# A decoder layer in fp32: two groups of attention steps placed later in a written schedule

## The chip, the cores and the metric

The kernel runs on one core of one Trainium2 chip. The metric is the device time of one execution in microseconds (us): the median of several runs. The core has five engines that run beside each other and wait for one another by semaphores: TensorE (PE, with its weight loads as PEld), VectorE (DVE), ScalarE (ACT), GpSimd (POOL) and SyncE (SP), which here issues nearly all of the transfers.

## The reference

One layer of a decoder on 512 tokens of width 2048, all in fp32:

```
h    = rms_norm(x, norm1_g)
proj = h @ w_in                     # split into aq ak av | bu bg | cq ck cv
out_a = dilated_mixture(rms(aq), rms(ak), av)       # 8 heads x 64, three (window, dilation) patterns
out_b = conformer_conv(bu, bg, ...)                 # GLU, causal conv of 31, layer norm, silu
out_c = band_attention(rms(cq), rms(ck), cv, 127, sinks)   # 16 query heads, 2 kv heads, x 64
x = x + concat(out_a, out_b, out_c) @ w_out
h2 = rms_norm(x, norm2_g)
x = x + (silu(h2 @ w_gate) * (h2 @ w_up)) @ w_down
```

Both attentions are softmax(q k) v with a mask. The C heads see a window of 128 tokens and have a sink in the denominator. The A heads see all 512 tokens through one mask whose entries count how many of the three patterns hold a pair.

## The kernel before

Every fp32 product is made of three products of split operands: high times high, high times low, low times high. A weight comes in by DMA, ACT rounds it to its high part (wh, line 289), and DVE subtracts to get its low part (wl, line 263).

The work goes in stages: the input projection (30 column tiles, named in the list PROJ), the output projection (16 tiles in two halves of the rows, ROWS), and the feed-forward part, which takes most of the time. The attention and the convolution are not stages of their own. They are strewn over the input projection and the first half of the output projection, so that PE has the projection's matmuls to do while the other engines work on the heads.

What is strewn where is written out by hand with a counter of ticks. The class Ticks keeps a list of functions due at each tick. project() calls ticks.tick() after every two steps of the contraction, that is after every six matmuls, so a column tile has eight ticks; a tile of the first half of the output projection has four. Each tick issues what is due at it, in the order in which it was entered, into the queues of the engines. Every engine then works through its own queue in that order. A step that is due a tick later thus stands behind some six more matmuls in PE's queue, and behind what the other engines were given in that tick.

The function attention(kind, box, mix, mi, heads) enters the steps of two heads for each query tile. Its distances in ticks come from the two tuples C_TICKS and A_TICKS, unpacked in one line:

```python
ready, every, step, s1, sx, s2, fl, ev, we = C_TICKS if kind == "c" else A_TICKS
if mi in ROWS[-2:]:
    fl, we = fl + 2, we + 3
at_v = (len(us) - 1) * step + s1 + sx + s2 + fl + len(TBANKS[kind]) - 1 + ev + EV + we
t0 = max(ticks.now + ready, head_at[0], box["q at"] - s1, box["k at"], box["v at"] - at_v)
ticks.after(tu + s2 + fl, packed_flip)        # C
ticks.after(tu + s2 + fl + t, flip, t)        # A, t = 0, 1, 2
ticks.after(t0 + at_v, weigh)
```

A head starts at t0, and the next one `every` ticks later: six for C, eight for A. The steps of a head are:

- scores (lines 814 and 815): q times k, on PE, in two (C) or three (A) PSUM banks, `step` ticks apart
- pack or top (820 to 829, 880 to 883): masks and maxima, on DVE; then exps (835, 889) on ACT and the norm (842 to 844, 896 to 900) on DVE
- flip: PE turns the normed weights, four 128x128 blocks at once for a C head (850) and 4, 4 and 2 blocks in three successive ticks for an A head (916)
- high and low: for an A head ACT casts the turned bank (922) and DVE subtracts (927); for a C head ACT and DVE do the same (856, 861), and POOL then selects the band out of both parts into four tiles ph and pl (870 and 873)
- weigh: PE multiplies with v, from ph (940) and pl (941), eight matmuls a head, into one bank
- out_high and out_rows: ACT copies one half of that bank (949) and DVE adds the other (954), one and two ticks after weigh

When both heads of a row are done, split_mix makes its high part on ACT (994) and its low part on DVE (995). The C rows are split at ticks that are set by the projection's last tiles; a row that ends after the projection is split one tick after its out_rows. For all heads but two, t0 is set by the head before or by q; for none is it set by v.

Two shared stores matter. PSUM has six banks for the scores, turns and products of all heads, and two ("tiles") for the projection's own tiles. SBUF has a pool of 73 slots of 128x512 (sp, N_SLOTS) for nearly every tile of a head. A slot is taken at the first write of a tile and given back at its last read; the next tile to be written gets the slot that came back first. If none is free, the writing engine waits for one. In the output projection the bank of a tile is freed by residual() (line 1073, xr), one tick after the tile's end.

Of the kernel before, what the change touches and what calls it, by code (L numbers as in the profile page):

```python
# [39 lines left out]
SD, KD, VD, EV = 9, 6, 12, 1  # L40


C_TICKS = (1, 6, 2, 2, 2, 3, 5, 1, 4)
A_TICKS = (0, 8, 2, 1, 3, 1, 3, 1, 5)


PROJ = ("bu0 bg0 bu1 bg1 cv ck cq0 bu2 cq3 cq1 cq5 bu3 cq2 bg2 cq7 "
# [69 lines left out]
def kernel(ctx: ExitStack, tc: tile.TileContext, xT, wi, wo, wgu, wd, cst_in, outT):  # L117
# [675 lines left out]
    def attention(kind, box, mix, mi, heads):  # L793
        ready, every, step, s1, sx, s2, fl, ev, we = C_TICKS if kind == "c" else A_TICKS

# [898 lines left out]
```

## Time and profile before

| | us |
|---|---|
| median of 3 runs | 1843.22 |
| lowest and highest run | 1843.0 and 1843.69 |
| profiled execution, its own time | 1845.39 |
| profiled execution, span from first to last instruction | 1843.6 |

| engine | busy us | share of the span |
|---|---|---|
| PE | 1835.2 | 100% |
| PEld | 1522.4 | 83% |
| DVE | 1445.8 | 78% |
| ACT | 1312.1 | 71% |
| POOL | 1026.2 | 56% |

The granted TensorE clock is 1.00. The attention lies between about 100 and 470 us of the span, the feed-forward part after 580 us.

A row of a timeline has the start and the length in us, the engine, the line, the operation, the tiles (out<-in) with their shapes, the number of instructions, and in brackets the idle time just before it with what ended it. c1o is the product with v of row c1, c1ph and c1pl its operands, a0t a turned bank of row a0, a0e its normed weights; digits of heads are left out, so both heads of a row have the same name. Matmuls overlap, so the time that one takes from the next is the distance of their starts, not the length of the row. A row of the waits has the waiting engine, tile and line, what it waited for, the sum in us, how often, and the longest.

### The profile page before, as it was taken

What the parts mean: (1) busy time and instruction counts of PE and PEld (TensorE: products, weight loads), DVE (VectorE), ACT (ScalarE), POOL (GpSimd) and SP (SyncE); (2) the same over time, 40 slices, a digit from 0 to 9 for tenths busy, and PEclk for the clock granted to TensorE, in tenths of its full rate; (3) what the DMA queues carried; (4) which work ended last, traced back from release to release, by engine and by line L of the source; (5) the groups of instructions that cost most, each with busy time, mean ns of one, the idle gap of its engine ahead of it and who ended that gap; (6) DMA issues with size and microseconds to landing.
All of it is one profiled execution on the core that took longest, in us unless ns stands there. A gap on an engine that the chain in (4) does not pass through costs nothing.

```text
span 1843.6 us, 26502 instructions
## 1 busy us (share of the span) xinstructions
PE 1835.2 (100%) x8314; PEld 1522.4 (83%) x8314; DVE 1445.8 (78%) x2063; ACT 1312.1 (71%) x1784; POOL 1026.2 (56%) x790
## 2 busy tenths in 40 slices
PE   9999999999999999999999999999999999999998
PEld 7888888888888888888888888888888888888887
DVE  6789988997689877778777787777777777777777
ACT  6345554553458788888888888888887778777775
POOL 0126644110003557886788767878676558776552
PEclk9999999999999999999999999999999999999999
DMA  7353345353343457677867778677687679877735
GB/s 276 87 150 93 87 121 153 107 161 116 124 149 103 115 151 191 188 213 182 225 187 200 201 188 226 181 209 199 182 273 258 204 225 295 257 254 260 240 119 110
DMA packets 398924, 334.61 MB, mean 181 GB/s; under 512 B 184256, under 2 KB 326720, under 8 KB 398784
## 3 DMA queue, kind: packets, MB, share of 16 engines
q1 hardware_dynamic: 398208, 332.14, 62.3%
q8 instruction: 66, 1.08, 0.3%
q10 hardware_dynamic: 576, 0.79, 0.1%
q14 instruction: 74, 0.61, 0.1%
HBM read 258.46 MB, written 65.98 MB: 176 GB/s over the span
## 4 chain that ended last, share of the span: by engine, by line
PE 95%; DVE 3%; DMA 1%; issue 0%; ACT 0%; SPq 0%; POOL 0%; DVEq 0%; POOLq 0%; ACTq 0%
PE out L1281 15%; PE out L1279 15%; PE out L1282 15%; PE out L1544 7%; PE out L1546 7%; PE out L1545 7%; PE o L322 3%; PE o L323 3%; PE o L324 3%; PE cq L322 2%; PE cq L324 2%; PE cq L323 2%; PE in L324 1%; PE in L323 1%; PE in L322 1%; PE aq L322 1%
## 5 line engine op out<-in xcount | busy, mean ns | idle before, releaser
L1279 PE MATMUL out<-wh,h 128*128 128x512 f32 x1232 | 479.2, 389 | 0.0
L1281 PE MATMUL out<-wl,h 128*128 128x512 f32 x1232 | 479.2, 389 | 0.0
L1282 PE MATMUL out<-wh,h 128*128 128x512 f32 x1232 | 479.2, 389 | 0.0
L1279 PEld LDWEIGHTS out<-wh,h 128*128 128x128 f32 x1232 | 231.2, 188 | 48.1
L1282 PEld LDWEIGHTS out<-wh,h 128*128 128x128 f32 x1232 | 231.2, 188 | 48.0
L1281 PEld LDWEIGHTS out<-wl,h 128*128 128x128 f32 x1232 | 231.2, 188 | 47.9
L1545 PE MATMUL out<-wl,a 128*128 128x512 f32 x620 | 240.4, 388 | 0.1
L1544 PE MATMUL out<-wh,a 128*128 128x512 f32 x620 | 240.4, 388 | 0.0
L1546 PE MATMUL out<-wh,a 128*128 128x512 f32 x620 | 240.3, 388 | 0.0
L289 ACT CAST wh<-w 128x1024 fp32r<-128x1024 f32 (+2 forms) x94 | 96.9, 1031 | 121.6 <-PE o L323 48.0
L1554 DVE TENSOR_TENSOR y<-y,out 128x512 f32<-128x512 f32 x192 | 128.5, 684 | 47.8 <-PE out L1546 46.1
L263 DVE TENSOR_TENSOR wl<-w,wh 128x1024 fp32r<-128x1024 f32 (+2 forms) x95 | 115.0, 1211 | 30.9 <-ACT wh L289 27.9
L1545 PEld LDWEIGHTS out<-wl,a 128*128 128x128 f32 x620 | 116.4, 188 | 24.5 <-DVE wl L285 0.5
L1546 PEld LDWEIGHTS out<-wh,a 128*128 128x128 f32 x620 | 116.4, 188 | 23.8
L1544 PEld LDWEIGHTS out<-wh,a 128*128 128x128 f32 x620 | 116.4, 188 | 23.8
L573 DVE SCALAR_TENSOR_TENSOR y<-bu,cst,y 128x511 f32<-128x511 f32 (+14 forms) x120 | 92.0, 767 | 1.3
L322 PE MATMUL o<-mh_c,wh 128*128 128x512 f32 x128 | 51.1, 399 | 0.2 <-DVE xr L1073 0.2
L322 PE MATMUL cq<-hh,wh 128*128 128x512 f32 x128 | 50.3, 393 | 0.0
L324 PE MATMUL o<-mh_c,wl 128*128 128x512 f32 x128 | 50.0, 391 | 0.0
L323 PE MATMUL o<-ml_c,wh 128*128 128x512 f32 x128 | 50.0, 390 | 0.0
L323 PE MATMUL cq<-hl,wh 128*128 128x512 f32 x128 | 49.9, 390 | 0.0
L324 PE MATMUL cq<-hh,wl 128*128 128x512 f32 x128 | 49.9, 390 | 0.0
(2351 smaller groups left out, 4766.5 us busy)
## 6 DMA issues: line engine op xcount, KB each, us to landing
od<-a SPq DMA_DIRECT2D x154, 256.0 KB
a<-od SPq DMA_DIRECT2D x154, 256.0 KB
w<-in_wi SPq DMA_DIRECT2D x58, 512.0 KB
w<-in_wo SPq DMA_DIRECT2D x32, 512.0 KB
x<-in_xT SPq DMA_DIRECT2D x16, 256.0 KB
xr<-in_xT SPq DMA_DIRECT2D x16, 256.0 KB
x2d<-xr SPq DMA_DIRECT2D x16, 256.0 KB
z<-x2d SPq DMA_DIRECT2D x64, 64.0 KB
```

Of the source, the lines that this page charges most:

```text
L263: fn(*args)
L289: (nc.vector.tensor_copy if u == 0 else nc.scalar.copy)(hi[:, :n], t[:, :n])
L322: nc.tensor.matmul(out, wh, xh, start=start, stop=False)
L323: nc.tensor.matmul(out, wh, xl, start=False, stop=False)
L324: nc.tensor.matmul(out, wl, xh, start=False, stop=stop)
L1279: nc.tensor.matmul(b, x[:, high], wh[:, s], start=c == f == 0 and q in (7, 1, 5, 2), stop=False, skip_group_check=True)
L1281: nc.tensor.matmul(b, x[:, high], wl[:, s], start=False, stop=False, skip_group_check=True)
L1282: nc.tensor.matmul(b, x[:, low], wh[:, s], start=False, stop=c == f == 1, skip_group_check=True)
L1544: nc.tensor.matmul(b[:, lo:hi], x[:, high], wh[:, s], start=start, stop=False, skip_group_check=True)
L1545: nc.tensor.matmul(b[:, lo:hi], x[:, high], wl[:, s], start=False, stop=False, skip_group_check=True)
L1546: nc.tensor.matmul(b[:, lo:hi], x[:, low], wh[:, s], start=False, stop=last, skip_group_check=True)
L1554: getattr(eng, op)(t, t, src)
```

## The change

Two figures of the two tuples change. The last one of C_TICKS, `we`, goes from 4 to 6: the products with v of every C head, and with them out_high and out_rows, come two ticks later. (The change was described as three steps; the diff has two.) The seventh of A_TICKS, `fl`, goes from 3 to 4: the three turns of every A head come one tick later, and so does all that is counted from them: high, low, weigh, out_high, out_rows. Nothing else is touched; scores, maxima, exponentials, norms, turns of the C heads and the selects on POOL keep their ticks.

```diff
-C_TICKS = (1, 6, 2, 2, 2, 3, 5, 1, 4)
-A_TICKS = (0, 8, 2, 1, 3, 1, 3, 1, 5)
+C_TICKS = (1, 6, 2, 2, 2, 3, 5, 1, 6)
+A_TICKS = (0, 8, 2, 1, 3, 1, 4, 1, 5)
```

## The prediction

> **What bounds the kernel now.** I read the page first, for the share of the engines and for the chain, then the list of waits on TensorE, then the stages, then TensorE's timeline around each wait.
>
> ```profile
> span 1843.6 us, 26502 instructions
> PE 95%; DVE 3%; DMA 1%; issue 0%; ACT 0%; SPq 0%; POOL 0%; DVEq 0%; POOLq 0%; ACTq 0%
> ```
>
> The chain of waits lies on TensorE (PE) for 95% of the span, so only time in which PE stands still can be won, and only a new standstill of PE can cost. The whole list of what PE waited for is short:
>
> ```profile
> PE idle L348 <- DVE nhalf L352: 1.1, 1, 1.1
> PE c1o L941 <- POOL c1pl L873: 0.8, 2, 0.5
> PE sides L1509 <- DVE y L1523: 0.6, 1, 0.6
> PE in L516 <- ACT hh L402: 0.6, 1, 0.6
> PE a0t L916 <- DVE a0e L900: 0.3, 1, 0.3
> PE o L322 <- DVE xr L1073: 0.2, 1, 0.2
> PE a1t L916 <- DVE a1e L900: 0.2, 1, 0.2
> ```
>
> "idle" and "in" are the start and "sides" is the end of the kernel; no moved step is near them. The other four lie in the attention, and three of them are waits of steps that the change moves: the products with v of one C head (c1o) and the turns of two A heads (a0t, a1t). The fourth, "o", waits for a residual addition of DVE. The stage says why DVE is late there:
>
> ```profile
> 299.00:403.00 104.00, 103.39 (x508) 86.36 (x506) 96.13 (x236) 54.50 (x97) 20.76 (x32) 1.00 0.51 135
> ```
>
> The columns are length, then the busy time of PE, weight loads, DVE, ACT and POOL, the granted clock, DMA. Where the A heads begin (299 to 403 us), DVE, the fourth figure, works 96.13 of 104.00 us, so whatever DVE hands to PE there comes late.
>
> **The change part by part.** No instruction is added or removed. The words of the change say three steps for the C heads; the diff raises the last figure from 4 to 6, two ticks, and I go by the diff. For each of 16 C heads two ticks later come 8 products on PE, one copy on ACT (L949), one addition on DVE (L954). For each of 8 A heads one tick later come 10 turns on PE, three casts on ACT (L922), three subtractions on DVE (L927), then the 8 products, their copy and addition, and for a1, a2 and a3, which end late, the split of the row (L994, L995). None of these issues a DMA, so nothing is moved on SP's queue; on POOL nothing is moved either, but slots that POOL writes come free later (below). The scores, maxima, exponentials and norms keep their ticks.
>
> *The C products.* PE's timeline at both heads of c1:
>
> ```profile
> 183.55 0.28 PE L940 MATMUL c1o<-c1ph,cv 128*128 128x256 f32 x1
> 184.34 0.39 PE L941 MATMUL c1o<-c1pl,cv 128*128 128x256 f32 x1 [0.52 <-POOL c1pl L873]
> ...
> 185.77 0.45 PE L322 MATMUL cq<-hh,wh 128*128 128x512 f32 x1
> ...
> 195.41 0.28 PE L940 MATMUL c1o<-c1ph,cv 128*128 128x256 f32 x1
> ...
> 196.30 0.45 PE L322 MATMUL bg<-hh,wh 128*128 128x512 f32 x1
> ```
>
> The first head's group takes 185.77 - 183.55 = 2.22 us, the second's 196.30 - 195.41 = 0.89. The loss is 1.33 us, more than the 0.8 of the list, since that list leaves out the pipeline's refilling. The two heads lie six ticks apart: (195.41 - 183.55 - 1.33) / 6 = 1.75 us for a tick. What was late is POOL:
>
> ```profile
> 182.91 1.39 POOL L873 TENSOR_SCALAR_AFFINE_SELECT c1pl<-c1lp 128x256 fp32r<-128x256 f32 x1
> 184.25 0.82 POOL L870 TENSOR_SCALAR_AFFINE_SELECT c1pl<-c1lp 128x256 fp32r<-128x256 f32 x1
> 185.03 0.29 POOL L873 TENSOR_SCALAR_AFFINE_SELECT c1pl<-c1lp 128x128 fp32r<-128x128 f32 x1
> ```
>
> POOL's last select ends at 185.03 + 0.29 = 185.32. Two ticks later the group would start at 183.55 + 3.50 = 187.05, 1.7 us after that. So the 1.33 us go: **-1.33**. Next late would be the second head of the same pair, which already runs without a wait. The copy and the addition behind the products are needed only when the rows are split, over 20 ticks later for every C row by the code's times; that cover hides them. If it were gone, they would cost one ACT and one DVE instruction each.
>
> One of the selects took 1.39 us, its neighbour of the same size 0.82. The row that overlaps it is DVE's split of a weight, with both inputs in SBUF:
>
> ```profile
> 182.63 1.40 DVE L263 TENSOR_TENSOR wl<-w,wh 128x1024 fp32r<-128x1024 f32 x1 [0.20 <-ACT wh L289]
> ```
>
> The select ends at 184.30, 0.27 us after the split's end at 184.03. The Trainium skill, page "SBUF — State Buffer", section "Who interferes with whom", says that a VectorE instruction with two SBUF inputs keeps a GpSimd instruction that reads SBUF out altogether until it is through; these two rows agree. By that rule the selects' length depends on what DVE runs beside them and can change with any change of the alignment; what it would do here is the third rival.
>
> *The A turns.* First an undisturbed group of turns with the scores behind it, then the two late ones:
>
> ```profile
> 331.88 0.60 PE L916 MATMUL a0t<-ident,a0e 128*128 128x128 f32 x4
> 332.24 0.48 PE L814 MATMUL a0s<-ak0h,aq 128*128 128x512 f32 x1
> 332.56 0.39 PE L815 MATMUL a0s<-ak0l,aq 128*128 128x512 f32 x1
> 332.79 0.40 PE L322 MATMUL av<-hh,wh 128*128 128x512 f32 x1
> ...
> 345.23 0.49 PE L916 MATMUL a0t<-ident,a0e 128*128 128x128 f32 x3
> 346.00 0.33 PE L916 MATMUL a0t<-ident,a0e 128*128 128x128 f32 x1 [0.28 <-DVE a0e L900]
> 346.09 0.48 PE L814 MATMUL a1s<-ak1h,aq 128*128 128x512 f32 x1
> ...
> 374.21 0.49 PE L916 MATMUL a1t<-ident,a1e 128*128 128x128 f32 x3
> 374.88 0.33 PE L916 MATMUL a1t<-ident,a1e 128*128 128x128 f32 x1 [0.17 <-DVE a1e L900]
> 374.96 0.48 PE L322 MATMUL aq<-hh,wh 128*128 128x512 f32 x1
> ```
>
> Four turns take 332.24 - 331.88 = 0.36 us to the next start; at 345.23 they take 0.86 and at 374.21 0.75. The losses are 0.50 and 0.39, because PE arrives up to half a microsecond before the last norm. A tick later (1.75 us) PE arrives well over 1 us after it: **-0.89**. A cover that shrinks: the turned banks are freed by DVE's subtractions a tick later, while the scores that use the six banks next keep their ticks. No wait for a bank stands in the list now, so its cost lies between nothing and one tick (1.75); I take nothing, because the list of PE's waits has no row of that kind (for the same reason there is nothing to gain), and keep the tick for the range. Splitting a turn from the scores it shared a tick with costs little: the joint group takes 332.79 - 331.88 = 0.91. I allow 0.02 us for each of some ten new groups, from the resolution of these rows: **+0.2**.
>
> *The residual.* The bank that output tile 2 needs is freed by xr:
>
> ```profile
> 402.46 0.39 PE L815 MATMUL a2s<-ak2l,aq 128*128 128x512 f32 x1
> 403.05 0.47 PE L322 MATMUL o<-mh_c,wh 128*128 128x512 f32 x1 [0.20 <-DVE xr L1073]
> ```
>
> ```profile
> 397.90 0.69 DVE L995 TENSOR_TENSOR ml_a<-mix_a,mh_a 128x512 fp32r<-128x512 f32 x1 [0.69 <-ACT mh_a L994]
> ```
>
> The step to the next matmul is 0.59, against 332.79 - 332.56 = 0.23 undisturbed: a loss of 0.36. DVE stood 0.69 us idle ahead of ml_a, the split of row a1, which the change puts a tick later: behind the weight's split and the norm, in front of xr still. ACT's cast for it is then ready in time, DVE loses its 0.69 idle, and xr comes earlier by that. Bounds: all of the 0.36 goes, or ml_a stays late and xr comes a tick (1.75) later. I take most of it, **-0.3**, the row's 0.69 being larger than what is needed.
>
> Sum: -1.33 - 0.89 - 0.3 + 0.2 = -2.3 us. The profiled execution took 1845.39 us (span 1843.6 and 1.79 around it), so its like would take 1843.1. The median of the runs, 1843.22, is 2.17 lower; there the sum gives **1840.9 us**, 0.13% less. More than 1.33 + 0.89 + 0.36 = 2.58 us is not to be had by this change, as the list has no other wait of PE in the attention.
>
> **The rivals.**
>
> *Slots (slower).* 73 slots serve the C parts, the A exponentials and the q, k, v copies. A slot goes to the next writer in the order in which slots come free, and around the last C head and the first A head they run out:
>
> ```profile
> 328.42 0.78 ACT L889 ACTIVATE a0e<-a0s,a0d,aq0r 128x512 f32<-128x512 f32 x1 [3.90 <-PE c6o L940]
> ```
>
> ```profile
> 330.51 0.48 DVE L900 TENSOR_SCALAR a0e<-a0e,a0d 128x512 f32<-128x512 f32 x1
> ```
>
> The exponentials of A head 0 stood 3.90 us until the products of c6 freed a slot, not because they read those products. The change holds four slots and a half of v for two ticks longer just there. If the same writer gets the same slot, ACT starts 3.5 us later, DVE's norm (ending at 330.99 now) ends at 334.5, and the turns, at 331.88 + 1.75 = 333.63, wait 0.9; DVE, with no slack up to 403, carries the rest of its 3.5 us on to the later turns and to xr. PE then loses about 3.5 in that stage in place of 1.25, so the time is 1843.22 - 1.33 + 2.25 + 0.2 = 1844.3; with two writers held, 7 us instead of 3.5, 1847.8. It decides from the point where the added hold is over 2 us. Against it: counting through the code's ticks, the copy of the moved products (L949) also takes its slot two ticks later, and the freed copy of q (after L681) comes ahead of the products, so that the exponentials would get that one and wait less. For it: the count leaves one or two free slots.
>
> *Hidden already.* If DVE's 96 of 104 us set the pace there, PE's earlier arrival by 1.33 us only lengthens its later waits, and the shifted turns wait for the next norm instead. Then 1843.22 - 1.33 + 1.33 - 0.3 = 1842.9. For it: the chain passes through DVE for 3% of the span, most of it here. Against it: the waits there sum to 1.25 us and a tick is 1.75.
>
> *POOL falls back again.* Should DVE's two-input work meet two selects of one head, each grown from about 0.4 to 1.39 and more, the two ticks would still leave 1.7 us of room; about 1 us of c1o's wait at another head would remain: 1841.9.
>
> **How the numbers follow.** Forecast (1840.4 to 1841.6) 0.50; POOL 0.10; hidden already 0.14; slots 0.20, of which 0.11 is above 1846.9; a gain that I don't see 0.06. The predicted time is that of the forecast, 1840.9. The range leaves out what is beyond the single hold at the top, and at the bottom reaches to the 2.58 us and the runs' own spread (1843.0 to 1843.69): 1839.9 to 1844.4. About what a measurement of this kernel can tell from no change is 0.2%, 3.7 us, so faster means below 1839.5 and slower above 1846.9: faster 0.06, the same 0.83, slower 0.11.
>
> **What would show it.** Right: the rows for c1o, a0t and a1t are gone from PE's waits, c1o's first group takes 0.89 us, xr's wait is under 0.1, and PE's busy time in 100 to 403 us is all of the stage. Wrong: a new row of PE waiting for DVE's a0e or a1e, or for a weight's split, or ACT's a0e waiting on c6o for over 4 us; or the four waits gone and the time still at 1843, which would mean that DVE carried the loss on to a place I don't name.

## The result, and the profile after

The kernel is slower. The median after is 1849.56 us (1847.53 to 1851.35), beside 1843.69 (1842.93 to 1845.19) for the kernel before on the same chip: a ratio of 1.0032, 95% interval 1.002 to 1.0044, or 5.9 us where I had forecast a gain of 2.3.

The profiled execution took 1849.91 us (span 1848.2). A part of the difference between two executions lies at the start: the products of line 322 begin at 10.18 us in the profile before and at 8.14 in that of the A turns alone (below), though nothing that is moved comes near them. So I compare a stretch that leaves the start out: from the first product of cv to the last one of the first half of the output projection. Its two ends in the timeline of TensorE (PE), before:

```profile
51.01 0.39 PE L322 MATMUL cv<-hh,wh 128*128 128x512 f32 x1
...
580.05 0.39 PE L324 MATMUL o<-mh_a,wl 128*128 128x512 f32 x1
```

and after:

```profile
49.92 0.39 PE L322 MATMUL cv<-hh,wh 128*128 128x512 f32 x1
...
584.62 0.39 PE L324 MATMUL o<-mh_a,wl 128*128 128x512 f32 x1
```

The stretch was 580.05 - 51.01 = 529.04 us and is 584.62 - 49.92 = 534.70: **5.66 us** more. Of these, 5.37 are lost up to the first product of the output projection (389.23 before, 393.51 after), that is in the attention. The list of PE's waits, after:

```profile
PE a1s L814 <- DVE a0pl L927: 1.9, 1, 1.9
...
PE a1s L814 <- DVE mix_c L954: 0.7, 1, 0.7
...
PE c6o L941 <- POOL c6pl L873: 0.6, 1, 0.6
PE a0t L916 <- DVE a0e L900: 0.5, 1, 0.5
...
PE lv L472 <- DVE lnv L412: 0.4, 1, 0.4
```

The rows for c1o, a1t and o, which the change was to remove, are gone, and the one for a0t is of another turn. So five new waits stand in their place, and four of them lie in the stage where DVE has no time to spare. That stage, with the columns of the prediction's row:

```profile
299.00:403.00 104.00, 100.14 (x484) 82.94 (x484) 94.80 (x233) 53.20 (x96) 22.42 (x32) 0.98 0.48 129
```

PE's busy time went from 103.39 to 100.14, DVE's from 96.13 to 94.80 in the same 104 us: both did less, so something kept both from working. The timelines of POOL, ACT, DVE and PE around row c6 tell what, after:

```profile
330.05 0.41 POOL L870 TENSOR_SCALAR_AFFINE_SELECT c6pl<-c6lp 128x256 fp32r<-128x256 f32 x1 [5.11 <-PE c6o L941]
...
330.12 0.58 ACT L949 COPY mix_c<-c6o 64x512 f32<-64x512 f32 x1 [5.68 <-PE c6o L941]
330.73 0.78 ACT L889 ACTIVATE a0e<-a0s,a0d,aq0r 128x512 f32<-128x512 f32 x1
...
330.74 0.69 DVE L681 TENSOR_TENSOR aq1l<-aq1raw,aq 128x512 fp32r<-128x512 f32 x1 [4.56 <-POOL c6pl L873]
...
329.88 0.28 PE L940 MATMUL c6o<-c6ph,cv 128*128 128x256 f32 x1
330.76 0.39 PE L941 MATMUL c6o<-c6pl,cv 128*128 128x256 f32 x1 [0.60 <-POOL c6pl L873]
...
334.05 0.33 PE L916 MATMUL a0t<-ident,a0e 128*128 128x128 f32 x1 [0.50 <-DVE a0e L900]
```

Three engines stood for some five microseconds, and the row of each of these stands names the products of c6 (c6o) or their operand c6pl. Yet DVE's subtraction aq1l <- aq1raw, aq reads nothing of c6: it makes the low half of a q. What it needs from c6 is a slot to write to, and by its row that slot comes back with POOL's last select. The second tile of the low part of c6's second head (c6pl) took its slot only when the first products of that same head had given one back. The products had been moved two ticks away (from 326.32 to 329.40 us, 3.1 us here), so POOL stood until then, ACT's copy into mix_c too, and DVE stood behind POOL for 4.56 us. Its row before:

```profile
328.33 0.69 DVE L681 TENSOR_TENSOR aq1l<-aq1raw,aq 128x512 fp32r<-128x512 f32 x1 [0.91 <-POOL c6pl L873]
```

It had stood 0.91 us. After the change PE then waited for the low part that it had itself held up, and at 334.05 for DVE's norm.

DVE stays late by what it lost, and two more waits follow from that, with something new behind the longer one. PE's timeline, after:

```profile
358.07 0.39 PE L324 MATMUL aq<-hh,wl 128*128 128x512 f32 x1
360.32 0.45 PE L814 MATMUL a1s<-ak1h,aq 128*128 128x384 f32 x1 [1.86 <-DVE a0pl L927]
...
360.78 0.60 PE L322 MATMUL aq<-hh,wh 128*128 128x512 f32 x1
...
364.42 0.40 PE L322 MATMUL aq<-hh,wh 128*128 128x512 f32 x1
```

The scores of a1 wait for a PSUM bank that a late subtraction (a0pl) frees: 360.32 - 358.07 = 2.25 us in place of 0.23. Then nine products take 364.42 - 360.78 = 3.64 us, where nine of 0.23 take 2.05: for 3.6 us the array ran at about half its pace, up to 0.43 us for a product. The granted clock of the stage, 0.98 in the row above, says the same.

### The profile page after: what moved, and what is told of

Same layout as the page of the kernel before. It is cut to its first block, busy times and chain, and to the rows that moved or that the text cites. A ratio compares the mean times of both kernels' runs of the same rounds, so it can differ in the third digit from the quotient of the medians.

```text
span 1848.2 us, 26504 instructions
## 1 busy us (share of the span) xinstructions
PE 1836.9 (99%) x8314; PEld 1522.2 (82%) x8314; DVE 1446.4 (78%) x2063; ACT 1313.0 (71%) x1784; POOL 1029.1 (56%) x790
## 4 chain that ended last, share of the span: by engine, by line
PE 73%; DVE 1%; DMA 0%; issue 0%; ACT 0%; DVEq 0%; SPq 0%
PE out L1282 15%; PE out L1279 15%; PE out L1281 15%; PE out L1545 7%; PE out L1544 7%; PE out L1546 7%; PE o L322 2%; PE o L324 2%; PE o L323 2%; DVE y L1554 0%; DVE wl L285 0%; DMA out_T<-z 0%; DVE z L1453 0%; DVE lnv L412 0%; DVE y L1523 0%
```

## The experiments

The table has the results of all runs; the stretch is read as above, from each profile. In the variants that add lines to the code, the lines behind them have numbers higher by two or three. A cut of code shows only the changed lines. "Before" is the kernel before on the same chip.

| kernel | median us | before | ratio, 95% interval | stretch us | against 529.04 |
|---|---|---|---|---|---|
| the change | 1849.56 | 1843.69 | 1.0032, 1.002 to 1.0044 | 534.70 | +5.66 |
| A turns alone | 1844.68 | 1843.96 | 1.0, 0.9991 to 1.0009 | 528.40 | -0.64 |
| C products alone | 1849.75 | 1843.96 | 1.0033, 1.002 to 1.0045 | 533.33 | +4.29 |
| change, c6 put back | 1843.14 | 1843.96 | 0.9998, 0.9989 to 1.0007 | 528.16 | -0.88 |
| change, 74 slots | 1850.19 | 1843.96 | 1.0035, 1.0023 to 1.0048 | 534.00 | +4.96 |
| before, c6 two ticks later | 1849.44 | 1843.79 | 1.0032, 1.0021 to 1.0043 | 532.90 | +3.86 |
| C alone, PE kept busy | 1850.11 | 1843.79 | 1.0033, 1.0021 to 1.0046 | 533.75 | +4.71 |
| before, 72 slots | 1845.44 | 1843.79 | 1.0009, 1.0 to 1.0018 | 529.70 | +0.66 |
| before, c6 one tick later | 1845.81 | 1843.94 | 1.0007, 0.9998 to 1.0016 | 530.03 | +0.99 |
| before, c6 three ticks later | 1843.23 | 1843.94 | 0.9999, 0.999 to 1.0008 | 528.29 | -0.75 |
| change, c6 a tick later still | 1848.81 | 1843.68 | 1.0026, 1.0017 to 1.0036 | 534.63 | +5.59 |
| a mended version, first | 1842.2 | 1843.79 | 0.9993, 0.9984 to 1.0002 | 526.75 | -2.29 |
| a mended version, again | 1841.47 | 1843.94 | 0.9988, 0.9979 to 0.9997 | 526.88 | -2.16 |

The theory after the result was: slots, with DVE's stand as the way from POOL to PE. The rival was banks: the A turns come a tick later while the scores keep their place, so the scores run out of banks by themselves.

**The two parts apart.** C's distance alone, and A's alone, both against the kernel before.

```diff
-C_TICKS = (1, 6, 2, 2, 2, 3, 5, 1, 4)
+C_TICKS = (1, 6, 2, 2, 2, 3, 5, 1, 6)
```

> Only the C products come two ticks later; the A turns are as in the kernel before. Slots theory (row c6 holds its four operands and v two ticks longer, POOL's last low select waits for c6's own first products, DVE stands behind it): DVE's aq1l still waits some 4.5 us for POOL's c6pl, PE's a0t waits grow to 1.5 us and more because the turns are not later, and the time is 1845 to 1849. Banks theory (the turned A heads run out of PSUM banks): PE's a1s does not wait, c1o's 1.33 us are won, 1842 to 1843.

```diff
-A_TICKS = (0, 8, 2, 1, 3, 1, 3, 1, 5)
+A_TICKS = (0, 8, 2, 1, 3, 1, 4, 1, 5)
```

> Only the A turns come a tick later; the C products are as in the kernel before. Slots theory: DVE's aq1l waits about 1 us as before, the a0t and a1t waits are gone, c1o's 1.33 us stay: 1842 to 1843. Banks theory: PE's a1s waits 1 to 2.6 us for DVE and the clock falls behind it: 1845 to 1848.

The C products alone lose as much as both (1.0033), a little more than the 1845 to 1849 us of the expectation, and the A turns alone lose nothing (1.0); their 1844.68 us are not the 1842 to 1843 that I expected, so their gain of 0.64 us in the stretch can't be told in the median. PE's waits in the C run, in 100 to 480 us:

```profile
PE a0t L916 <- DVE a0e L900: 2.4, 1, 2.4
PE c6o L941 <- POOL c6pl L873: 0.6, 1, 0.6
```

DVE's stand, and PE's products behind its wait:

```profile
332.21 0.69 DVE L681 TENSOR_TENSOR aq1l<-aq1raw,aq 128x512 fp32r<-128x512 f32 x1 [4.58 <-POOL c6pl L873]
...
337.08 0.63 PE L323 MATMUL av<-hl,wh 128*128 128x512 f32 x1
337.51 0.63 PE L324 MATMUL av<-hh,wl 128*128 128x512 f32 x1
```

No score waits for a bank there, and yet the loss is there, with the same stand of DVE. In the A run no score waits either. So banks are not the cause. They are a place where the loss comes out once DVE is late: with the A turns a tick later PE meets the bank before it meets the turn.

**Row c6.** The change with c6's products where they were, and the kernel before with c6's products alone two ticks later. The cut is of the first; the second has we + 2 in the same place:

```diff
+        if mi == "c6":
+            we = we - 2
```

> Both parts as in the change, but the products of the one row c6, the last C row, keep their old distance (4 ticks instead of 6). Slots theory: no standstill of DVE's aq1l over 1 us, none of a1s, c1o's wait gone: 1840.5 to 1841.8. Banks theory: a1s waits as in the change, 1845 to 1849.

> The kernel before, with the products of the single row c6 two ticks later and nothing else moved. If that row's slots are the whole cause: POOL's c6pl waits 4 to 6 us for c6's own products, DVE's aq1l 4 to 5 us behind it, a0t over 2 us with half the clock behind it, and since c1o's 1.33 us are not won either the time is 1849.5 to 1852. If the other seven C rows share the loss: under 1847.

One row of eight carries it: 1.0032 with c6 alone, 0.9998 without it; in the stretch, 3.86 us of the 4.29 of all C rows. With c6 alone, DVE's row and PE's two:

```profile
330.22 0.69 DVE L681 TENSOR_TENSOR aq1l<-aq1raw,aq 128x512 fp32r<-128x512 f32 x1 [5.71 <-POOL c6pl L875]
...
333.53 0.33 PE L918 MATMUL a0t<-ident,a0e 128*128 128x128 f32 x1 [2.38 <-DVE a0e L902]
...
348.50 0.33 PE L918 MATMUL a0t<-ident,a0e 128*128 128x128 f32 x1 [1.39 <-DVE a0e L902]
```

DVE's stand grew by 5.71 - 0.91 = 4.8 us; PE's waits there are 2.38 + 1.39 + 0.6 (c6's own) = 4.4, in place of one of 0.28 before, and the stretch is 3.86 us longer. What DVE loses there, PE pays for the most part.

With c6 put back the attention has no wait of PE left, but the time did not fall to the 1840.5 to 1841.8 that I expected; that was a miss. The whole list of PE's waits in that run:

```profile
PE idle L348 <- DVE nhalf L352: 1.1, 1, 1.1
PE sides L1511 <- DVE y L1525: 0.6, 1, 0.6
PE in L516 <- ACT hh L402: 0.6, 1, 0.6
PE lv L472 <- DVE lnv L412: 0.3, 1, 0.3
```

The row of lv is new. It belongs to the convolution's layer norm, whose sums DVE prepares (lnv) behind its y at line 603. DVE's timeline there, before, and in this run:

```profile
472.06 2.48 DVE L603 SCALAR_TENSOR_TENSOR y<-lnm,y 128x512 f32<-128x512 f32 x4 [2.00 <-PE lnm L601]
...
475.66 2.28 DVE L412 TENSOR_TENSOR lnv<-lnv,lq 128x512 f32<-128x512 f32 x3
```

```profile
470.35 2.48 DVE L603 SCALAR_TENSOR_TENSOR y<-lnm,y 128x512 f32<-128x512 f32 x4 [5.29 <-PE lnm L601]
472.86 0.69 DVE L956 TENSOR_TENSOR mix_a<-mix_a,a3o 64x512 f32<-64x512 f32 x1
...
475.29 2.29 DVE L412 TENSOR_TENSOR lnv<-lnv,lq 128x512 f32<-128x512 f32 x3 [0.36 <-ACT lq L411]
```

The addition for row a3 (mix_a), moved a tick, now stands between the two; ACT's cast of that row waits for it and puts off the squares (lq) that lnv reads. So lnv follows y by 4.94 us in place of 3.60. PE stands 0.3 us for it, and loses 0.5 until its next start. The A run has the same row, and the C run, where a3 keeps its tick, has not.

**The number of slots.** The change with one more slot, and the kernel before with one less.

```diff
-N_SLOTS = 73
+N_SLOTS = 74
```

> The change with 74 slots instead of 73, all that SBUF has room for. Slots theory: the standstill of POOL's c6pl and of DVE's aq1l shrinks from 4.6 to under 2 us if one slot is what is missing, and the time falls to 1841 to 1844; if two are missing it stays at 1847 or more. Banks theory: no change, 1849.

```diff
-N_SLOTS = 73
+N_SLOTS = 72
```

> The kernel before with 72 slots instead of 73 and no step moved. Slots theory: the pool runs out around the same place, waits of POOL's c6ph or c6pl, ACT's a0e and DVE's aq1l grow by 1 to 4 us, and the time is 1845 to 1850. If the tick of the products matters and not the number of slots: no change, 1843.5 to 1844.5.

One slot more does not help (1.0035). It moves the hold: POOL has its slot, and DVE now waits for c6's release itself. The slots of the whole attention are dealt anew, too. Of the 4.96 us, 1.02 are lost before a0's first score, where one score of c2 and two of c7 now stand 0.8, 0.2 and 0.2 us behind DVE; from there on this kernel loses 3.94 us, and the change 6.14. One slot less costs the kernel before 0.66 us of the stretch (1.0009, just at the edge of what is measured), with the same instruction late. DVE's row with 74 slots, with PE's longest wait there and two products behind it, and DVE's row with 72:

```profile
333.01 0.69 DVE L681 TENSOR_TENSOR aq1l<-aq1raw,aq 128x512 fp32r<-128x512 f32 x1 [4.26 <-PE c6o L941]
...
362.59 0.44 PE L814 MATMUL a1s<-ak1h,aq 128*128 128x384 f32 x1 [1.92 <-DVE a0pl L927]
...
363.05 0.39 PE L322 MATMUL aq<-hh,wh 128*128 128x512 f32 x1
363.28 0.40 PE L323 MATMUL aq<-hl,wh 128*128 128x512 f32 x1
```

```profile
328.74 0.70 DVE L681 TENSOR_TENSOR aq1l<-aq1raw,aq 128x512 fp32r<-128x512 f32 x1 [1.90 <-PE c6o L941]
```

So at this place several claims stand in line for the slots of c6, and the kernel before had none to spare.

**The length of the hold, or the order.** If the loss were simply the length of the hold, it would grow with c6's distance. The kernel before with c6's products one tick later, and three:

```diff
+        if mi == "c6":
+            we = we + 1
```

> The kernel before with row c6's products one tick later instead of two. If DVE's stand in front of the low half of q is the cause and DVE has no slack to pay it from, the stand grows from 0.91 us by about one tick, to 2.7, TensorE loses about 1.2 us of it (in the run with two ticks the stand grew by 4.8 us and the time up to the layer norm by 4.2), and the time is 1.2 to 2 us above before. If there is a threshold, because a slot is still free for that one tick, DVE's stand stays near 0.9 and the time is that of before within 0.5 us.

> The kernel before with row c6's products three ticks later. By the stand of DVE: it grows by another tick over the run with two, from 5.71 to about 7.4 us, and the time by another 1.5 to 1.75, to 7 to 7.5 us above before. By the rival that the products as such got late (they would be later than something that reads them), the step from two to three would be more than a tick.

One tick costs 0.99 us of the stretch, two cost 3.86, and three cost nothing: -0.75. (By the medians it is 1.9, 5.7 and -0.7; the interval for one tick, 0.9998 to 1.0016, still touches no change.) The expectation of a stand that grows by a tick each time was wrong, and with it the simple form of my theory: the time with one tick came out as expected by luck, since DVE stood 0.91 us at aq1l as before and lost its time elsewhere. The rows say why. With one tick:

```profile
330.21 0.78 ACT L891 ACTIVATE a0e<-a0s,a0d,aq0r 128x512 f32<-128x512 f32 x1 [4.07 <-PE c6o L942]
...
331.02 0.69 DVE L898 SCALAR_TENSOR_TENSOR a0e<-a0e,mult_a 128x512 f32<-128x512 f32 x1 [1.84 <-ACT a0e L891]
```

With three:

```profile
321.77 0.62 POOL L872 TENSOR_SCALAR_AFFINE_SELECT c6ph<-c6hp 128x256 fp32r<-128x256 f32 x1 [6.27 <-PE c6o L943]
...
325.97 0.69 DVE L681 TENSOR_TENSOR aq1l<-aq1raw,aq 128x512 fp32r<-128x512 f32 x1 [0.28 <-POOL c6pl L875]
```

With one tick the claim that meets c6's second head is the exponential of a0, as it was in the kernel before (3.90 us there), only later; with two it is c6's own low part; with three the selects of the second head wait 6.27 us for the first head's products, which costs nothing, since POOL has that time, and find their slots there, so that nobody waits for the second head. As I read these rows, each claim is tied to one release by the order in which both stand in the program, and a tick more changes the partners.

The same with the A turns moved as well (we + 1 for c6 on top of the change):

> The change as it is, and row c6's products one tick later still (three ticks later than before). If the loss is a matter of which claim meets which release, as the run with c6 alone three ticks later says, the self-wait of c6's low part is gone, DVE's stand in front of the low half of q is under 1 us, the long waits for a0pl and mix_c are gone, and the time is that of the change with c6 put back, 1843.1, within 1 us. If the length of the hold costs, the stand grows by a tick over the change's 4.56 us and the time is 1851 or more. Between the two, the A turns' new places could make another claim wait: then 1845 to 1848, with a row of its own on ACT, DVE or POOL.

It did not mend the change: 1.0026, between the two times that I had set against each other. The partners are others again. DVE isn't held at aq1l, but ACT and POOL are, by scores of a0, DVE then for 2.83 us by ACT's exponential, and PE at the end by a bank:

```profile
331.04 0.62 ACT L677 CAST aq<-aq1raw 64x512 fp32r<-64x512 f32 x1 [4.70 <-PE a0s L816]
...
331.30 0.41 POOL L872 TENSOR_SCALAR_AFFINE_SELECT c6pl<-c6lp 128x256 fp32r<-128x256 f32 x1 [11.05 <-PE a0s L817]
...
345.94 0.69 PE L816 MATMUL a1s<-ak1h,aq 128*128 128x384 f32 x1 [3.47 <-DVE mix_c L956]
```

**The half pace.** In the run with C alone, too, products came at 0.43 us (337.51 - 337.08) after PE's stand of 2.4 us. Is that a part of the loss? The C kernel with ten more products in the place where PE stands; they are written into the bank of a0's first turn, which then writes over them:

```diff
+                if mi == "a0" and h == 0 and t == 0:
+                    for _ in range(10):
+                        nc.tensor.matmul(b, h_hi[0][:, :P], h_hi[0], start=True, stop=True, skip_group_check=True)
```

> The kernel with only the C products later, and ten extra matmuls of 128x512 into the bank of a0's first turn, ahead of the turn that waits 2.4 us: TensorE works through that time instead of standing still; the extra products are overwritten by the turn. If the slower clock behind the wait costs the difference between 0.43 and 0.23 us a matmul for some 12 matmuls (2.5 us): the clock stays at full speed, the steps behind the turn are 0.23 us, and the time falls from 1849.8 to 1847 to 1847.8. If the slow steps come from something other than the standstill: no fall, 1849.5 to 1852.

PE's timeline and its waits in that run:

```profile
331.99 2.51 PE L915 MATMUL a0t<-hh 128*128 128x512 f32 x10
334.34 0.87 PE L919 MATMUL a0t<-ident,a0e 128*128 128x128 f32 x4
```

```profile
PE a0t L919 <- DVE a0e L900: 1.4, 1, 1.4
PE a1t L919 <- DVE a1e L900: 0.7, 1, 0.7
```

The stand is filled, and the products behind it come at 0.23 us again. But the time did not fall (1.0033): PE is back sooner and waits for DVE further on, 1.4 us at the next head's turn and 0.7 at a1's. In this kernel the half pace covers waits that would come anyhow, because DVE sets the pace there. The run with c6 alone says the same, since its profile has no half pace and 3.86 us of loss. In the change itself it did cost, as far as two profiles can tell: with 74 slots the same score stood 1.92 us, the products behind it came at 0.23 us, and PE's waits further on are no longer than in the change. There the 1.6 us of the half pace were simply not lost.

**A version that is faster.** Against the kernel before: C one tick later in place of two, c6 where it was, A's turns a tick later, and the layer norm's work a tick later, so that its sums do not meet a3's addition:

```diff
-T_LN = 250
+T_LN = 251
-C_TICKS = (1, 6, 2, 2, 2, 3, 5, 1, 4)
-A_TICKS = (0, 8, 2, 1, 3, 1, 3, 1, 5)
+C_TICKS = (1, 6, 2, 2, 2, 3, 5, 1, 5)
+A_TICKS = (0, 8, 2, 1, 3, 1, 4, 1, 5)
+        if mi == "c6":
+            we = 4
```

> A candidate: C products one tick later instead of two, those of c6 at their old distance, the A turns one tick later as in the change, and the layer norm's steps one tick later too, so that they keep their order against row a3. Slots theory: no standstill of aq1l over 1 us, c1o's wait down to 0.5 us or none, the turns' waits gone, no wait of lv: 1841.0 to 1842.5. If the banks or the layer norm lose it again: 1843 to 1844.

> The kernel with C products one tick later, c6 where it was, A turns one tick later and the layer norm's work started a tick later, again, with more rounds, since its interval touched no change by 0.0002: if its four removed waits and its lack of a new one are worth what the trace says (2.0 us from the first full product to a place behind the layer norm), the ratio is 0.9989 to 0.9995 and its interval excludes 1.

```profile
PE idle L348 <- DVE nhalf L352: 1.1, 1, 1.1
PE in L516 <- ACT hh L402: 0.7, 1, 0.7
PE sides L1511 <- DVE y L1525: 0.6, 1, 0.6
```

This is the whole list of PE's waits in the second of the two runs. None is left in the attention, the stretch is 2.2 us shorter, and the time is 1841.47 us, 0.12% below before (0.9988, 0.9979 to 0.9997). The first run's interval still held no change (0.9984 to 1.0002). The four parts were not run apart in this form.

## Why the prediction was wrong, step by step

*The step that failed* is the one that priced the moved products by PE's row alone and argued the slots away: "the freed copy of q (after L681) comes ahead of the products, so that the exponentials would get that one and wait less". It did not come to that. The copy of q came free at 331.43 us, when L681 had run, and the exponentials had begun at 330.73. They waited for no slot themselves, but stood on ACT behind the moved copy into mix_c, which had waited 5.68 us for one, and began 3.4 us later after cv's first product than before (280.8 in place of 277.4). I had followed one claim, and others stood ahead of it: that copy, c6's own low part, and the low half of the next q itself, the instruction whose end was to free the copy of q. What the runs showed in its place is DVE's stand of 4.56 us at that instruction (0.91 before), which PE then paid for. The rival "Slots (slower)" happened, at 0.20 of the chance, and with the price of its case of two holds, 1847.8, nearer to the 1849.56 than that of one. The nearness is luck, since it held the exponentials and not DVE's subtraction. Its point of decision, a hold of over 2 us, was wrong as well: three ticks more (5.25 us by the tick of 1.75) cost nothing, and one tick cost 0.99 us of the stretch. What decides is which claim meets which release.

*The C products, -1.33.* The row of c1o is gone and its group takes 0.89 us, as forecast. But up to the first score of a0 the stretch got only 0.5 us shorter with the change, with C alone and with c6 put back alike (0.9 to 1.1 with one tick, in the mended version). A part went to c7's scores, which now come late behind the turns of c2, after:

```profile
222.70 0.60 PE L850 MATMUL c2t<-ident,c2e 128*128 128x128 f32 x4
223.39 0.36 PE L814 MATMUL c7s<-ckh,cq 128*128 128x256 f32 x1
```

This step took 0.35 us before and takes 0.69; at the other head of c2 it went from 0.36 to 0.54. That is 0.5 us; the other 0.3 I have not found.

*The A turns, -0.89.* Right: with A alone, the time from the first product of cv to the first of the output projection falls from 338.22 to 337.30 us, 0.92, and no turn waits.

*The residual, -0.3.* The wait of o is gone: the step takes 0.23 us in place of 0.59. But it is gone in all other runs too, also where a1's split keeps its tick (0.23 with c6 alone and with 72 slots, 0.26 with c6 three ticks later, where PE comes no later than before). So my reason for it is not shown. And of the instructions moved behind it I followed only the split of a1. The addition of a3, moved too, fell between y and lnv and gave some 0.5 us back. This was a term that I had not written down.

*The bank, "between nothing and one tick; I take nothing".* Nothing was right as long as DVE is in time. With DVE late it was more than my upper bound: 1.13 and 2.25 us at two scores in place of 0.23 each (the first at 343.13 us, the second shown above), 2.9 us together. I had bounded it as if DVE's subtractions could be late by the tick alone.

*New groups, +0.2*: too small to be seen beside the rest.

*POOL falls back again* did not happen: no row of c1o is left. *Hidden already* held in one respect. In that stage DVE does set the pace as soon as it has lost something: filling PE's stand brought nothing in the C kernel.

The sum for the change by rows: c6's own group 0.9 (1.75 us in place of 0.88), a0t's first turns 0.7, the turns of a0's second head 0.4 (0.72 us, with 0.36 undisturbed), the two banks 2.9, the half pace 1.6, lv 0.5 and c7's scores 0.5 make 7.5; less 1.33 + 0.89 + 0.36 for what was removed, that is 4.9 of the 5.66 us. The other 0.8 I have not followed; no row of the list of waits has them.

What stays open: the profile has no numbers of slots, so the partners are read from the releasers. And the medians lie higher than the profiles of the same runs say, 5.65 us beside 3.86 for c6 alone; executions of one kernel differ by up to 4 us, by the start and, it seems, by whether the half pace sets in.

## What to carry to other kernels

When tiles come from one pool, a reader moved later is also a writer moved later, on any engine, of a tile that has nothing to do with it; look for an instruction whose wait names a tile that it does not read. Count the claims and releases of the pool in program order around the moved step, for every claim and not just the most likely, and try one tick more or less before you believe a gain or a loss: here the same step at one, two and three ticks cost 1.0, 3.9 and nothing. Where the engine in the middle is nearly full, what it loses is paid at the next places where PE needs it, and filling one of them with work does not get it back.

## What the runs showed of the hardware that I had not expected

The array fell to half its pace after short stands. After 1.86 us in the change nine products took 0.43 us each at most; after 3.47 us in the last variant of c6 eleven did; after 2.38 us in the C run some ten did. After the same 2.38 us in the run with c6 alone none did, and none after 1.92 us in the run with 74 slots. The Trainium skill, page "TensorE: Matmul & The Clock Gate", section "What's actually happening", puts the fall to half clock after an idle window of about 3.4 us. These rows agree on the half pace, and differ on the time: 1.86 us was enough once, and 2.38 us was not always. The half pace made PE lose 1.6 us more behind the stand of 1.86 us (3.64 in place of 2.05) and 2.2 more behind that of 3.47 (4.67 in place of 2.50); what decides whether it sets in, no run here shows.
